# Passage to the feed-forward of a hybrid trunk layer: its sums and low parts on VectorE, recorded behind the scaling of the last row tile

## The chip, the cores and the metric

The kernel runs on one core of a Trainium2 chip. The metric is the device time of one execution in microseconds (us). The trace names the engines PE (TensorE matmul), PEld (TensorE weight load), DVE (VectorE), ACT (ScalarE), POOL (GpSimd) and SP (SyncE, which here issues the DMAs). Each engine works through its own list of instructions in order; an instruction that waits for another engine holds back all that stands behind it in its own list.

## What is computed

One trunk layer on x, 1024 rows (tokens) by 1024 columns, float32. Two mixers run first (a differential attention and an mLSTM); then comes the part that matters here:

```python
x = x + jnp.concatenate([attn_out, mlstm_out], axis=-1) @ w_out[l]

h2 = rms_norm(x, ffn_norm_g[l])
x = x + (jax.nn.silu(h2 @ w_gate[l]) * (h2 @ w_up[l])) @ w_down[l]
return rms_norm(x, final_norm_g)
```

The "passage" is the stretch from the last row tiles of `x + ... @ w_out` to the first products of `h2 @ w_gate` and `h2 @ w_up`.

## The kernel before

Every float32 product is made of three matmuls on two halves: a "high part" (the float32 value cast to float32r, a copy on ACT, L107) and a "low part" (the value less its high part, a subtraction, L108). `split(hi, lo, src, eng)` emits the two; `eng` is the engine of the subtraction, DVE unless POOL is named.

**Row tiles.** The 1024 rows are 8 tiles of 128. The output projection `out_proj` takes them in the order 0, 1, 2, 3, 4, 7, 6, 5. For each tile it runs 48 matmuls of 128x512 (24 into each half of the columns, tile name `dwo`, L1111 to L1113), adds x on DVE (`x1`, L1117), squares and sums the row on ACT (L1137), takes the reciprocal root on POOL (`ssq`, L1138, and `rs`, L104), and scales the row on DVE (`h2`, L1141). PE then transposes `h2` (L1047) into the operand of the feed-forward; DVE (L1053) and ACT (L1056) take the transposed tile out of PSUM with the norm's gain. For tile 5, the last, the transposes are named `th2l` and stand in PE's list behind the first 24 matmuls of the feed-forward.

**The feed-forward's first product is a seven-product scheme** (Strassen-Winograd, `unit`). With the transposed `h2` cut into four blocks (columns in halves, rows in halves), its seven right-hand operands are b11 and b21 (rows 0 to 511), b22 and b12 (rows 512 to 1023) and sums t1 = b12-b11, t3 = b22-b12, t2 = b22-t1 and t4 = b21-t2. Each is 128x4x512 and needs a high and a low part. Blocks of rows 0 to 511 are in `hst`, of rows 512 to 1023 in `h2r`.

- `t_slices(c)` makes the 128-row slice c of t1, t3 and b22 as soon as row tile c+4 is transposed: two subtractions on DVE (`tt`, `h2r`) and three splits (five DVE-sized instructions in all, and three ACT copies). Tiles 4, 7, 6 and 5 give slices 0, 3, 2 and 1.
- `t_sums(c)` turns slice c of `hst` into t2 and t4 in place, with two instructions.
- For the first two slices made (0 and 3; `TP = 2`) the low parts and the sums are on POOL; so are two of four low parts of b21 (`B21 = 2`) and those of t4.

**The units.** `unit` runs seven steps on a weight tile `st`: step 1 uses b11, 2 b21, 5 t1, 6 t2, 7 t3, 4 t4, 3 b22. A step is 12 matmuls (`mul12`, L186 to L188), and needs its weights split too (`w`) and, for some, sums of weight quarters on DVE (`st`, L214 to L235). The first two units (gate and up, `two`) are interleaved, so a step takes 24 matmuls: first step 1 of both, then the transposes `th2l`, then steps 2 and 5 of both, and so on. A matmul of step 5 reads all 512 columns of t1, which is all four slices.

**What sets the order.** PE's list is written by hand here (`manual_schedule`). The lists of DVE, ACT and POOL are set by a scheduler that places each instruction where it expects the engine to be free; `tc.high_priority()` moves instructions ahead, and `tc.issue_after(i)` keeps instructions behind instruction i.

Of the kernel before, what the change touches and what calls it, by code (L numbers as in the profile page):

```python
# [14 lines left out]
ALU = mybir.AluOpType  # L15
# [16 lines left out]
ML_K = 128 ** -0.5  # L32
RING, RING_A, RING_F = 9, 5, 7
AHEAD = 2
TP = 2
B21 = 2
XT = 4
M_POOL = (1, 2)
UO = (0, 1, 3, 2, 4, 5, 6, 7)
# [16 lines left out]
LATE = (10, 13, 6, 9)  # L56
# [3 lines left out]
LAST = DONE[-1]  # L60
SLICES = [i - 4 for i in DONE if i >= 4]
# [3 lines left out]
def block_kernel(ctx, tc, x, xT, pos, cols, gate_b, lam_in, w_vg, w_mo, w_qk, w_dv,  # L65
                 w_out, w_gu, w_dn, fng, out):
    nc = tc.nc
    act, dve, pool, pe, sp = nc.scalar, nc.vector, nc.gpsimd, nc.tensor, nc.sync
# [37 lines left out]
    def split(hi, lo, src, eng=None):  # L106
        act.copy(hi, src)  # L107
        (eng or dve).tensor_sub(lo, src, hi.bitcast(F32))  # L108
# [14 lines left out]
    def ring_tile(ringb, n_all, n=512):  # L123
        i = ring_n[0] % n_all
        ring_n[0] += 1
        w = (ringa if i < RING_A else ringb).tile([P, 2, 520], F32R, tag="w", name="w")
        return w[:, 0, 0:n], w[:, 1, 0:n]
# [27 lines left out]
    def drain(gen):  # L155
        for _ in gen:
            pass
# [230 lines left out]
    with ExitStack() as pa:  # L388
# [3 lines left out]
        with ExitStack() as pm:  # L392
# [80 lines left out]
            for n in range(4):  # L473
                for a in range(2):
# [5 lines left out]
            t1, t2, t3 = ([tq.tile([P, 4, 512], F32R, tag=f"t{n}{hl}", name=f"t{n}{hl}") for hl in range(2)]  # L480
                          for n in (1, 2, 3))
# [529 lines left out]
        while not done:  # L1011
            u, st = next(steps)
# [8 lines left out]
    b12, b22 = h2r  # L1021
    pb = ctx.enter_context(ExitStack())
    bw = pb.enter_context(tc.tile_pool(name="b_work", bufs=2, reuse_waits="tile"))
    H, hst, late_c, td_pool = {}, [], [], [psd]

    def t_slices(c):
        cs = slice(c * P, (c + 1) * P)
        p1, p2 = b12[:, :, cs], b22[:, :, cs]
        tt = bw.tile([P, 4, P], F32, tag="tt", name="tt", bufs=1)
        dve.tensor_sub(tt, p1, hst[0][:, :, cs])  # L1030
        eng = pool if c in SLICES[:TP] else dve
        split(H["t1"][0][:, :, cs], H["t1"][1][:, :, cs], tt, eng)
        dve.tensor_sub(p1, p2, p1)
        split(H["t3"][0][:, :, cs], H["t3"][1][:, :, cs], p1, eng)
        split(H["b22"][0][:, :, cs], H["b22"][1][:, :, cs], p2, eng)

    def t_sums(c):
        cs = slice(c * P, (c + 1) * P)
        eng = pool if c in SLICES[:TP] else dve
        eng.tensor_tensor(hst[0][:, :, cs], hst[0][:, :, cs], b12[:, :, cs], op=ALU.add)  # L1040
        eng.tensor_tensor(hst[1][:, :, cs], hst[1][:, :, cs], hst[0][:, :, cs], op=ALU.subtract)

    def h2_out(i, h2, ps_tile, gs=(0, 1)):
        for g in gs:
            tp = ps_tile()
            for j in range(4):
                pe.transpose(tp[:, j, :], h2[:, (4 * g + j) * P:(4 * g + j + 1) * P], ident)  # L1047
            if i < 4:
                dst = bw.tile([P, 4, P], F32, tag="tt", name="ht", bufs=1)
            else:  # L1050
                dst = h2r[g][:, :, (i - 4) * P:(i - 3) * P]
            if g == 0:
                dve.tensor_tensor(dst, tp, gffn[:, 0:4].unsqueeze(2).broadcast_to([P, 4, P]), op=ALU.mult)  # L1053
            else:
                for j in range(4):
                    act.mul(dst[:, j], tp[:, j], gffn[:, 4 + j:5 + j])  # L1056
            if i < 4:
                sp.dma_start(h2_d[g][:, :, i * P:(i + 1) * P], dst)
                n_h2[0] += 1
        if i >= 4 and 1 in gs:  # L1060
            if hst:
                t_slices(i - 4)
            else:
                late_c.append(i - 4)

    def d_tile():
        return td_pool[0].tile([P, 4, P], F32, tag="d", name="td")

    def out_proj():
        prev = nxt = None  # L1070

        def load(i):
            mt = bw.tile([P, 8, P], F32, tag="mt", name="mt", bufs=1)
            mf = mt.rearrange("p h e -> p (h e)")
            sp.dma_start(mf[:, 0:256], mx_da[i])
            if i != LAST:
                sp.dma_start(mf[:, 256:512], mx_db[i])
            sp.dma_start(mf[:, 512:1024], mx_ml[:, i, :])
            x1 = bw.tile([P, S], F32, tag="x1", name="x1")
            sp.dma_start(x1, x[i * P:(i + 1) * P, :])  # L1080
            return [i, x1, mt, {}, 0, tm[0]]

        def poll():
            nonlocal nxt
            if nxt is None:
                if ready:
                    nxt = load(ready.pop(0))
                return
            nxt[4] += 1
            if nxt[4] in nxt[5][:2]:  # L1090
                g = 1 if nxt[4] == nxt[5][0] else 0
                tp = d_tile()
                for j in range(4):
                    src = mt_last[:, j - 2, :] if nxt[0] == LAST and 4 * g + j in (2, 3) else nxt[2][:, 4 * g + j, :]
                    pe.transpose(tp[:, j, :], src, ident)
                nxt[3][g] = [v.rearrange("p (j e) -> p j e", e=P) for v in ring_tile(None, RING_A)]
                split(*nxt[3][g], tp)

        while True:
            poll()  # L1100
            if nxt is None or nxt[4] < nxt[5][1]:
                yield 0 if nxt is None else None
                continue
            (i, x1, _, mm, _, th), nxt = nxt, None
            for u in range(2):
                us = slice(u * 512, (u + 1) * 512)
                ps = psd.tile([P, 512], F32, tag="d", name="dwo")
                for n_, k in enumerate((4, 5, 6, 7, 0, 1, 2, 3)):
                    mh, ml = (v[:, k % 4, :] for v in mm[k // 4])
                    wh, wl = (wo[hl, k // 4, u][:, k % 4] for hl in range(2))  # L1110
                    pe.matmul(ps, mh, wh, start=(n_ == 0), stop=False)  # L1111
                    pe.matmul(ps, mh, wl, start=False, stop=False)  # L1112
                    pe.matmul(ps, ml, wh, start=False, stop=(n_ == KC - 1))  # L1113
                    poll()
                    if n_ == KC - 1:
                        with tc.high_priority():
                            dve.tensor_add(x1[:, us], ps, x1[:, us])  # L1117
                    if prev and 8 * u + n_ in th[2:]:
                        g = th[2:].index(8 * u + n_)
                        h2_out(*prev, d_tile, (g,))  # L1120
                        if g:
                            prev = None
                            if i == LAST:
                                t_sums(SLICES[2])
                    yield
                if u == 0 and i == LAST:
                    for n, g in (("b11", 0), ("b21", 1)):
                        H[n] = [slots.tile([P, 4, 512], F32R, tag=f"A{hl}{g}", name=n) for hl in range(2)]
                        for q in range(4):
                            split(H[n][0][:, q], H[n][1][:, q], hst[g][:, q], pool if g and q < B21 else dve)  # L1130
                    for c in SLICES[:2]:
                        t_sums(c)
            ssq = bw.tile([P, 1], F32, tag="ssq2", name="ssq2")
            sp.dma_start(x1_d[i], x1)
            with tc.high_priority():
                h2 = bw.tile([P, S], F32, tag="h2", name="h2", bufs=1)
                act.activation(h2, x1, AF.Square, accum_out=ssq)  # L1137
                pool.tensor_scalar(ssq, ssq, 1.0 / S, EPS, op0=ALU.mult, op1=ALU.add)  # L1138
                rs = bw.tile([P, 1], F32, tag="rs", name="rs")
                rsqrt_of(rs, ssq)  # L1140
                dve.tensor_scalar_mul(h2, x1, rs)  # L1141
            prev = (i, h2)
            if i == LAST:
                out_last.append(prev)
                return

    out_last, tm, n_h2 = [], [(TM0, TM1) + TH], [0]
    f_ = out_proj()
    for u, st in steps:
        if st == 0:  # L1150
# [24 lines left out]
        sp.dma_start(hst[g], h2_d[g])  # L1175
    for c in late_c:
        t_slices(c)
    drain(f_)
    px.close()
    pps.close()  # L1180
# [40 lines left out]
        next(u)  # L1221
    with tc.high_priority():
        h2_out(*out_last[0], lambda: tl.pop())
    pb.close()
    ringc = ctx.enter_context(tc.tile_pool(name="ringc", bufs=RING_F - RING_A, reuse_waits="tile"))
    pfw = ExitStack()
    fw[0] = pfw.enter_context(tc.tile_pool(name="f_work", bufs=2, reuse_waits="tile"))
    for _ in range(2):
        for u in two:
            next(u)  # L1230
    t_sums(SLICES[3])
    for n, g in (("t2", 0), ("t4", 1)):
        H[n] = [slots.tile([P, 4, 512], F32R, tag=f"B{hl}{g}", name=n) for hl in range(2)]
        for q in range(4):
            split(H[n][0][:, q], H[n][1][:, q], hst[g][:, q], pool if g else dve)
    phs.close()
    ssp = ctx.enter_context(tc.tile_pool(name="ssp", bufs=1, side="right", reuse_waits="tile"))
    raw = {}
# [168 lines left out]
    for step in SEQ_D:  # L1407
        _, wq, q = STEP[step]
# [93 lines left out]
```

## Time and profile before

| | us |
|---|---|
| three runs | 1229.0, 1231.23, 1232.24 (median 1231.23) |
| the profiled execution, its own time | 1228.96 |
| its span in the trace | 1226.8 |

| engine | busy us | share of the span | instructions |
|---|---|---|---|
| PE | 1186.7 | 97% | 5692 |
| DVE | 862.2 | 70% | 1437 |
| ACT | 530.0 | 43% | 1114 |
| POOL | 276.6 | 23% | 212 |

The span runs from the first instruction to the last; 2.2 us of the execution lie around it. The passage lies between 530 and 600 us of the span. A time in a row is counted from the span's start. "Idle before" in brackets is how long the engine had nothing to do before an instruction, and behind the arrow is what ended it.

### The profile page before, as it was taken

What the parts mean: (1) busy time and instruction counts of PE and PEld (TensorE: products, weight loads), DVE (VectorE), ACT (ScalarE), POOL (GpSimd) and SP (SyncE); (2) the same over time, 40 slices, a digit from 0 to 9 for tenths busy, and PEclk for the clock granted to TensorE, in tenths of its full rate; (3) what the DMA queues carried; (4) which work ended last, traced back from release to release, by engine and by line L of the source; (5) the groups of instructions that cost most, each with busy time, mean ns of one, the idle gap of its engine ahead of it and who ended that gap; (6) DMA issues with size and microseconds to landing.
All of it is one profiled execution on the core that took longest, in us unless ns stands there. A gap on an engine that the chain in (4) does not pass through costs nothing.

```text
span 1226.8 us, 15931 instructions
## 1 busy us (share of the span) xinstructions
PE 1186.7 (97%) x5692; PEld 975.9 (80%) x5692; DVE 862.2 (70%) x1437; ACT 530.0 (43%) x1114; POOL 276.6 (23%) x212
## 2 busy tenths in 40 slices
PE   9899999899998999997999999999999999999997
PEld 7678877898886888886888888888888888888886
DVE  8667868854767767739866767676666778775674
ACT  4933344325557554735533233322333245344453
POOL 3145877401133100025121100111011102000000
PEclk9989999999999999999999999999999999999999
DMA  9368641421478334060132312323133268723241
GB/s 334 99 196 221 191 156 69 164 113 52 146 219 287 122 126 141 31 245 34 69 129 96 128 65 99 129 95 121 43 129 113 111 235 303 294 95 105 84 163 69
DMA packets 87727, 172.37 MB, mean 141 GB/s; under 512 B 10208, under 2 KB 43104, under 8 KB 81248
## 3 DMA queue, kind: packets, MB, share of 16 engines
q1 hardware_dynamic: 86032, 169.76, 40.4%
q10 hardware_dynamic: 1616, 1.59, 0.4%
q8 instruction: 45, 0.74, 0.2%
q14 instruction: 34, 0.28, 0.1%
HBM read 117.58 MB, written 53.74 MB: 140 GB/s over the span
## 4 chain that ended last, share of the span: by engine, by line
PE 77%; DVE 5%; POOL 5%; issue 5%; ACT 4%; DMA 4%; SPq 0%; ACTq 0%; POOLq 0%; DVEq 0%
PE g L186 13%; PE g L187 13%; PE g L188 13%; PE y L1419 6%; PE y L1418 6%; PE y L1420 6%; PE to L333 2%; PE dwo L1113 2%; PE dwo L1112 2%; PE dwo L1111 2%; DVE w L108 1%; PE s L290 1%; PE tat L325 1%; PE s L291 1%; DVE xt L583 1%
## 5 line engine op out<-in xcount | busy, mean ns | idle before, releaser
L107 ACT CAST w<-st 128x512 fp32r<-128x512 f32 x218 | 133.0, 619 | 272.2 <-PE g L188 121.9
L108 DVE TENSOR_TENSOR w<-st,w 128x512 fp32r<-128x512 f32 x203 | 160.8, 797 | 104.1 <-ACT w L107 103.0
L186 PE MATMUL g<-t,w 128*128 128x512 f32 x448 | 178.0, 397 | 0.0
L187 PE MATMUL g<-t,w 128*128 128x512 f32 x448 | 177.1, 395 | 0.0
L188 PE MATMUL g<-t,w 128*128 128x512 f32 x448 | 176.3, 393 | 0.0
L1419 PE MATMUL y<-fhl,w 128*128 128x512 f32 x308 | 122.0, 396 | 0.0
L1418 PE MATMUL y<-fhl,w 128*128 128x512 f32 x308 | 121.7, 395 | 0.0
L1420 PE MATMUL y<-fhl,w 128*128 128x512 f32 x308 | 120.8, 392 | 0.0
L187 PE MATMUL g<-b,w 128*128 128x512 f32 x264 | 104.8, 397 | 0.0
L186 PE MATMUL g<-b,w 128*128 128x512 f32 x264 | 104.2, 395 | 0.0
L188 PE MATMUL g<-b,w 128*128 128x512 f32 x264 | 104.0, 394 | 0.0
L186 PEld LDWEIGHTS g<-t,w 128*128 128x128 f32 x448 | 84.2, 188 | 22.9 <-DVE u L224 3.0
L188 PEld LDWEIGHTS g<-t,w 128*128 128x128 f32 x448 | 84.2, 188 | 20.3
L187 PEld LDWEIGHTS g<-t,w 128*128 128x128 f32 x448 | 84.3, 188 | 19.1
L1203 POOL TENSOR_TENSOR ss<-sg 128x512 f32<-128x512 f32 x11 | 17.3, 1575 | 354.5 <-DVE sg L1201 354.5
L107 ACT CAST w<-gs 128x512 fp32r<-128x512 f32 x76 | 46.5, 619 | 70.0 <-PE y L1420 52.3
L108 DVE TENSOR_TENSOR w<-gs,w 128x512 fp32r<-128x512 f32 x76 | 53.6, 712 | 29.5 <-ACT w L107 29.5
L1418 PEld LDWEIGHTS y<-fhl,w 128*128 128x128 f32 x308 | 57.8, 188 | 14.3
L108 DVE TENSOR_TENSOR fhl<-w,fhl 128x512 fp32r<-128x512 f32 x77 | 51.2, 698 | 25.5 <-ACT fhl L107 25.5
L1420 PEld LDWEIGHTS y<-fhl,w 128*128 128x128 f32 x308 | 57.9, 188 | 13.9
L1419 PEld LDWEIGHTS y<-fhl,w 128*128 128x128 f32 x308 | 57.9, 188 | 13.2
L107 ACT CAST fhl<-w 128x512 fp32r<-128x512 f32 x77 | 44.2, 618 | 45.4 <-PE y L1420 41.6
(358 smaller groups left out, 2666.7 us busy)
## 6 DMA issues: line engine op xcount, KB each, us to landing
st<-in_w_gu SPq DMA_DIRECT2D x22, 1024.0 KB
gs<-gm_d SPq DMA_DIRECT2D x76, 256.0 KB
gm_d<-sg SPq DMA_DIRECT2D x11, 1024.0 KB
w<-in_w_dn SPq DMA_DIRECT2D x44, 256.0 KB
gm_d<-ss SPq DMA_DIRECT2D x11, 768.0 KB
st<-in_w_qk SPq DMA_DIRECT2D x8, 1024.0 KB
qbuf<-q_d SPq DMA_DIRECT2D x64, 128.0 KB
q_d<-xt SPq DMA_DIRECT2D x24, 256.0 KB
```

The costliest lines, as they stand in the source:

```text
L107: act.copy(hi, src)
L108: (eng or dve).tensor_sub(lo, src, hi.bitcast(F32))
L186: pe.matmul(ps, w[0][:, ks], h[0][:, k, :], start=first and k == 0, stop=False, **sk)
L187: pe.matmul(ps, w[0][:, ks], h[1][:, k, :], start=False, stop=False, **sk)
L188: pe.matmul(ps, w[1][:, ks], h[0][:, k, :], start=False, stop=k == 3, **sk)
L333: pe.matmul(po[:, 0, :], at[:, j, :], dv[j // 4][:, j % 4, hh * P:(hh + 1) * P], start=(j == 0), stop=(j == i))
L1111: pe.matmul(ps, mh, wh, start=(n_ == 0), stop=False)
L1112: pe.matmul(ps, mh, wl, start=False, stop=False)
L1113: pe.matmul(ps, ml, wh, start=False, stop=(n_ == KC - 1))
L1418: pe.matmul(bk[q][b], gh, w[0], start=first and k == 0, stop=False, **sk)
L1419: pe.matmul(bk[q][b], gh, w[1], start=False, stop=False, **sk)
L1420: pe.matmul(bk[q][b], gl, w[0], start=False, stop=k == FH - 1, **sk)
```

## The change

Three things are changed, all in the passage.

- **Engines.** The 16 instructions of the passage that POOL had (low parts of slices 0 and 3, of two quarters of b21 and of t4, and the sums of slices 0 and 3) go to DVE.
- **Where slices are made.** While the last tiles are projected (`tm[0] == LATE`), `t_slices` is put off: the slices go into `late_c` and are emitted, with three `t_sums`, after `h2_out` of the last tile.
- **Order.** What is put off, and steps 2 and 5 of the first two units, are emitted under `tc.issue_after(scaled[0].ins)`: on each engine they stand behind the scaling of the last tile's rows (L1135 of the changed kernel).

```diff
@@ block_kernel @@
     def t_slices(c):
...
-        eng = pool if c in SLICES[:TP] else dve
-        split(H["t1"][0][:, :, cs], H["t1"][1][:, :, cs], tt, eng)
+        split(H["t1"][0][:, :, cs], H["t1"][1][:, :, cs], tt)
         dve.tensor_sub(p1, p2, p1)
-        split(H["t3"][0][:, :, cs], H["t3"][1][:, :, cs], p1, eng)
-        split(H["b22"][0][:, :, cs], H["b22"][1][:, :, cs], p2, eng)
+        split(H["t3"][0][:, :, cs], H["t3"][1][:, :, cs], p1)
+        split(H["b22"][0][:, :, cs], H["b22"][1][:, :, cs], p2)
     def t_sums(c):
         cs = slice(c * P, (c + 1) * P)
-        eng = pool if c in SLICES[:TP] else dve
-        eng.tensor_tensor(hst[0][:, :, cs], hst[0][:, :, cs], b12[:, :, cs], op=ALU.add)
-        eng.tensor_tensor(hst[1][:, :, cs], hst[1][:, :, cs], hst[0][:, :, cs], op=ALU.subtract)
+        dve.tensor_add(hst[0][:, :, cs], hst[0][:, :, cs], b12[:, :, cs])
+        dve.tensor_sub(hst[1][:, :, cs], hst[1][:, :, cs], hst[0][:, :, cs])
...
         if i >= 4 and 1 in gs:
-            if hst:
+            if hst and tm[0] != LATE:
                 t_slices(i - 4)
             else:
                 late_c.append(i - 4)
...
-                            if i == LAST:
-                                t_sums(SLICES[2])
                     yield
                 if u == 0 and i == LAST:
...
-                            split(H[n][0][:, q], H[n][1][:, q], hst[g][:, q], pool if g and q < B21 else dve)
-                    for c in SLICES[:2]:
-                        t_sums(c)
+                            split(H[n][0][:, q], H[n][1][:, q], hst[g][:, q])
...
-                dve.tensor_scalar_mul(h2, x1, rs)
+                scaled[0] = dve.tensor_scalar_mul(h2, x1, rs)
...
     with tc.high_priority():
         h2_out(*out_last[0], lambda: tl.pop())
+    with tc.issue_after(scaled[0].ins):
+        for c in late_c:
+            t_slices(c)
+        for c in SLICES[:3]:
+            t_sums(c)
...
     for _ in range(2):
         for u in two:
-            next(u)
+            with tc.issue_after(scaled[0].ins):
+                next(u)
     t_sums(SLICES[3])
...
-            split(H[n][0][:, q], H[n][1][:, q], hst[g][:, q], pool if g else dve)
+            split(H[n][0][:, q], H[n][1][:, q], hst[g][:, q])
```

The lists of PE and SP are the same in both kernels but for line numbers. What moved on POOL and DVE is shown here; names carry their buffer's number.

POOL's list around the last tile's `ssq2_5630` and `rs_5635` in the kernel before: b21's low parts, then the four sums of slices 0 and 3, then the reciprocal root of the last tile, then t4's low parts.

```order
L108 TENSOR_TENSOR b21_5571<-hst1_5277,b21_5570 128x512 x2
L1040 TENSOR_TENSOR hst0_5275<-hst0_5275,h2r0_3709 128x4x128 x2
L1041 TENSOR_TENSOR hst1_5277<-hst1_5277,hst0_5275 128x4x128 x2
L1138 TENSOR_SCALAR ssq2_5630<-ssq2_5630 128x1
L104 TENSOR_TENSOR rs_5635<-ssq2_5630,mhalf_110 128x1
L108 TENSOR_TENSOR t4_5793<-hst1_5277,t4_5792 128x512 x4
```

The same place in the changed kernel, from the tile before the last (`ssq2_5502`) to the first sums of the feed-forward's output (`ss`).

```order
L1132 TENSOR_SCALAR ssq2_5502<-ssq2_5502 128x1
L102 TENSOR_TENSOR rs_5507<-ssq2_5502,mhalf_110 128x1
L1132 TENSOR_SCALAR ssq2_5597<-ssq2_5597 128x1
L102 TENSOR_TENSOR rs_5602<-ssq2_5597,mhalf_110 128x1
L1198 TENSOR_TENSOR ss_5961<-sg_5952 128x512
```

Nothing of the passage but the reciprocal roots is left on POOL.

DVE's list in the kernel before, from the last addition of x (`x1_5430`) through the scaling of the last tile (`h2_5632`) to the low part of t1's last slice (`t11_5267<-tt_5698`, which step 5 needs).

```order
L1117 TENSOR_TENSOR x1_5430<-dwo_5584,x1_5430 128x512
L108 TENSOR_TENSOR t31_5269<-h2r0_3709,t30_5268 128x4x128
L108 TENSOR_TENSOR w_5747<-st_5645,w_5747 128x512
L1041 TENSOR_TENSOR hst1_5277<-hst1_5277,hst0_5275 128x4x128
L218 TENSOR_TENSOR st_5645<-st_5645 128x512
L1141 TENSOR_SCALAR h2_5632<-x1_5430,rs_5635 128x1024
L108 TENSOR_TENSOR w_5765<-st_5665,w_5765 128x512
L218 TENSOR_TENSOR st_5665<-st_5665 128x512
L1053 TENSOR_TENSOR h2r0_3709<-th2l_5644,colt_109 128x4x128
...
L1033 TENSOR_TENSOR h2r0_3709<-h2r1_3710,h2r0_3709 128x4x128
L108 TENSOR_TENSOR b221_5271<-h2r1_3710,b220_5270 128x4x128
L108 TENSOR_TENSOR t11_5267<-tt_5698,t10_5266 128x4x128
```

The same place in the changed kernel: the last low parts of b11, the last addition of x (`x1_5421`), the scaling (`h2_5599`), the first of what stands behind it, and the end of the row of slices.

```order
L106 TENSOR_TENSOR b11_5543<-hst0_5275,b11_5542 128x512 x4
L1115 TENSOR_TENSOR x1_5421<-dwo_5562,x1_5421 128x512
L1135 TENSOR_SCALAR h2_5599<-x1_5421,rs_5602 128x1024
L1028 TENSOR_TENSOR tt_5665<-h2r0_3709,hst0_5275 128x512
L106 TENSOR_TENSOR b221_5271<-h2r1_3710,b220_5270 128x4x128 x3
L106 TENSOR_TENSOR w_5714<-st_5612,w_5714 128x512
...
L1028 TENSOR_TENSOR tt_5692<-h2r0_3709,hst0_5275 128x512
L106 TENSOR_TENSOR t31_5269<-h2r0_3709,t30_5268 128x4x128
L1037 TENSOR_TENSOR hst1_5277<-hst1_5277,hst0_5275 128x4x128
L1030 TENSOR_TENSOR h2r0_3709<-h2r1_3710,h2r0_3709 128x4x128
L106 TENSOR_TENSOR t11_5267<-tt_5692,t10_5266 128x4x128
```

Between the scaling and t1's last low part, that low part counted in, stand 9 DVE instructions in the kernel before and 41 in the changed one; between the last addition of x and the scaling stand 4 before and none after. The 41 are 19 of the slices, 6 of `t_sums`, 8 sums of weight quarters, 7 low parts of weights and the taking out of `th2l`.

## Rows read from the trace of the kernel before

**Rows 1.** The page: busy time, share of the span, instructions.

```profile
PE 1186.7 (97%) x5692; PEld 975.9 (80%) x5692; DVE 862.2 (70%) x1437; ACT 530.0 (43%) x1114; POOL 276.6 (23%) x212
```

**Rows 2.** Waits of PE, 500 to 586: total us, times, longest.

```profile
PE th2l L1047 <- DVE h L1141: 5.3, 1, 5.3
PE td L1047 <- DVE h L1141: 1.1, 1, 1.1
```

**Rows 3.** Windows: stretch, us, busy by engine (instructions), PEclk, DMA share, GB/s.

```profile
570.00:580.00 10.00, 4.69 (x20) 3.81 (x20) 9.26 (x9) 3.73 (x8) 6.60 (x6) 0.86 0.13 52
586.00:700.00 114.00, 114.00 (x492) 91.98 (x491) 81.22 (x111) 38.15 (x65) 23.80 (x16) 1.00 0.29 107
```

**Rows 4.** Timeline of PE: start, us, engine, line, operation, count, idle before.

```profile
557.88 0.40 PE L1113 MATMUL dwo<-wo,w 128*128 128x512 f32 x1
559.39 0.63 PE L1047 MATMUL td<-ident,h 128*128 128x128 f32 x4 [1.11 <-DVE h L1141]
...
566.34 0.39 PE L1113 MATMUL dwo<-wo,w 128*128 128x512 f32 x1
...
571.92 0.39 PE L188 MATMUL g<-b,w 128*128 128x512 f32 x1
577.61 1.97 PE L1047 MATMUL th2l<-ident,h 128*128 128x128 f32 x8 [5.31 <-DVE h L1141]
579.23 0.78 PE L186 MATMUL g<-b,w 128*128 128x512 f32 x1
...
580.63 0.40 PE L186 MATMUL g<-b,w 128*128 128x512 f32 x1
...
585.75 0.39 PE L187 MATMUL g<-t,w 128*128 128x512 f32 x1
```

**Rows 5.** Timeline of POOL in the passage.

```profile
557.34 3.04 POOL L108 TENSOR_TENSOR b<-hst,b 128x512 fp32r<-128x512 f32 x2
566.42 5.79 POOL L1040 TENSOR_TENSOR hst<-hst,h2r 128x512 f32<-128x512 f32 x2 [6.04 <-DVE b L108]
572.17 3.38 POOL L1041 TENSOR_TENSOR hst<-hst,hst 128x512 f32<-128x512 f32 x2
575.64 0.51 POOL L1138 TENSOR_SCALAR ssq<-ssq 128x1 f32<-128x1 f32 x1
...
589.16 5.96 POOL L108 TENSOR_TENSOR t<-hst,t 128x512 fp32r<-128x512 f32 x4 [12.39 <-ACT t L107]
```

**Rows 6.** Timeline of ACT: the squares of the last tile's rows.

```profile
570.04 1.06 ACT L1137 ACTIVATE h<-x 128x1024 f32<-128x1024 f32 x1 [1.92 <-issue]
```

**Rows 7.** Timeline of DVE in the passage.

```profile
541.42 0.68 DVE L1117 TENSOR_TENSOR x<-dwo,x 128x512 f32<-128x512 f32 x1
544.29 0.75 DVE L1141 TENSOR_SCALAR h<-x,rs 128x1024 f32<-128x1024 f32 x1 [2.19 <-POOL rs L104]
...
557.48 1.77 DVE L1141 TENSOR_SCALAR h<-x,rs 128x1024 f32<-128x1024 f32 x1
...
569.27 0.68 DVE L1117 TENSOR_TENSOR x<-dwo,x 128x512 f32<-128x512 f32 x1
...
572.68 1.75 DVE L1041 TENSOR_TENSOR hst<-hst,hst 128x512 f32<-128x512 f32 x1
...
576.80 0.75 DVE L1141 TENSOR_SCALAR h<-x,rs 128x1024 f32<-128x1024 f32 x1 [0.71 <-POOL rs L104]
...
578.19 0.69 DVE L218 TENSOR_TENSOR st<-st 128x512 f32<-128x512 f32 x1
...
582.41 0.68 DVE L108 TENSOR_TENSOR t<-tt,t 128x512 fp32r<-128x512 f32 x1
...
588.43 0.68 DVE L108 TENSOR_TENSOR w<-st,w 128x512 fp32r<-128x512 f32 x1
```

**Rows 8.** Timeline of PE at the kernel's start: its first large matmuls.

```profile
5.12 0.79 PE L142 MATMUL po<-w,hT 128*128 128x512 f32 x1 [0.58 <-ACT hT L111]
...
10.40 0.47 PE L142 MATMUL po<-w,hT 128*128 128x512 f32 x1
```

More of the change, by code (lines that the diff above doesn't have):

```diff
@@ L34 @@
 AHEAD = 2
-TP = 2
-B21 = 2
 XT = 4
@@ L1067, in d_tile @@
         return td_pool[0].tile([P, 4, P], F32, tag="d", name="td")
+    scaled = [None]
     def out_proj():
@@ L1177, in block_kernel @@
         t_slices(c)
+    late_c.clear()
     drain(f_)
```

## The prediction

> **What bounds the kernel now.** The page comes first: PE is busy for 97% of the span [rows 1], so only time that PE loses or wins counts, and a wait of PE is paid in full. Next come PE's waits in the passage: two only, 5.3 us ahead of the last tile's transposes (`th2l`) and 1.1 us ahead of those of the tile before [rows 2]. From 586 to 700 PE has no idle time at all, 492 matmuls in 114 us, 0.232 us each [rows 3]; whatever is lost in the passage is not won back there.
>
> The timelines tell why PE waits. It is done with step 1 of the first two units at 572.3 (571.92 and 0.39) and goes on at 577.61 [rows 4]. The scaling that it waits for runs at 576.80 [rows 7]. The squares behind it were summed on ACT by about 571.2 [rows 6], but POOL, which takes the root, was in the four sums of `hst` from 566.42 until 575.55, and began `ssq` only at 575.64 [rows 5]. DVE had been late as well: the last matmul of the output projection ends at 566.73 [rows 4], and x is added at 569.27 [rows 7]. After the wait PE is slow: in the stretch 570 to 580 its granted clock is 0.86 [rows 3], and `th2l` and the next three matmuls take 3.02 us, 577.61 to 580.63 [rows 4].
>
> **What the change takes away.** POOL keeps nothing of the passage but the roots, and DVE nothing between the last addition of x and the scaling.
>
> The wait at tile 6 (1.11 us [rows 4]) was a scaling of 1.77 us instead of 0.75, beside POOL's b21 low parts [rows 5, 7]. With these gone from POOL, even from the same start, 557.48, it ends at 558.2, when PE's matmul of 557.88 ends too (558.3); I take the wait to go whole, and all of PE's later work to move 1.11 us ahead. The output projection then ends at 566.73 - 1.11 = 565.6.
>
> At the last tile an undisturbed passage is seen at tile 7: x is added at 541.42, the scaling starts at 544.29, ends at 545.04 [rows 7], which is 2.87 and 3.62 us later. So the changed kernel adds x at 565.7 and scales from 568.5 to 569.3. PE, done with step 1 at 572.3 - 1.11 = 571.2, finds `h2` ready; the 5.31 us go.
>
> The slow clock behind that wait goes too. The transposes took 1.62 us and the three matmuls 1.40 [rows 4]; at full clock the matmuls would take 3 x 0.232 = 0.70, and the transposes half, 0.81. That is 1.5 us.
>
> Together 1.1 + 5.3 + 1.5 = 7.9 us are won. PE would run `th2l` from 571.2 to 572.0 and step 2 of both units (24 x 0.232 = 5.6 us) until about 577.6; a weight's low part, fifth behind the scaling on DVE, may hold step 2 by 0.4 us, which the next wait swallows.
>
> **What it puts in.** Step 5 needs t1, high and low, of all four slices. Before, most of it was finished about when PE left the projection, and between the scaling and the last low part of t1 stood 9 DVE instructions, that one counted in; it ran at 582.41, and step 5 (its first low product at 585.75) came later than that and waited for nothing [rows 4, 7]. In the changed kernel 41 stand there. They are subtractions and additions of 128x512 float32, and the row that is nearest is DVE's own in the same passage: from 578.19 to 588.43 it ran 17 of the same kind back to back in 10.24 us, 0.602 each [rows 7], with POOL idle (12.39 us until 589.16 [rows 5]). That is also the cost of the 16 that come over from POOL, where they took 1.5 to 2.9 us each [rows 5]; off PE's path the change is a saving.
>
> The first of the 41 starts 0.7 us behind the scaling's start, at 569.2. The last starts 40 x 0.602 = 24.1 us later, at 593.3, and ends at 594.0. The first low product of step 5 then runs at 594.0 instead of 585.75: **8.3 us later**. PE stands still from 577.6 until then, 16.4 us, instead of 5.3, and must start from the slow clock as it did behind the 5.3. I take the same 1.5 us for that; the bounds are 0 and 2.5 (the kernel's first twelve large matmuls took 5.28 us, 5.12 to 10.40, where 2.8 is due [rows 8]).
>
> Check by the ledger: 16.4 + 1.5 - 7.9 = 10.0; by the clock times: 8.3 + 1.5 = 9.8. I take **+9.8 us**.
>
> Is anything late behind step 5? t2 stands 7 DVE instructions behind t1's last (4.2 us), under the 5.6 us of step 5; t3 is finished before that, and t4 (four instructions, formerly POOL's) is read three steps later. So no. Nothing is given back either: PE has no idle time there now [rows 3].
>
> Bounds of DVE's share: if every one of the 41 has to wait for a copy of ACT or a semaphore, each takes its whole 0.68 instead of 0.602 [rows 7], 3.2 us more; a gain below 0.602 has no row for two-operand work here, its case is the second rival. With the clock's bounds the forecast's own range is +8.3 to +14.
>
> **Rivals.** *The gain alone (faster).* The wait for t1 would have to be hidden: PE wins 7.9 us and the 16 instructions are cheaper on DVE. That gives 1228.96 - 7.9 = 1221.1 for the profiled execution, 1223.3 against the median. It decides on how many of the 41 must be done when step 2 ends at 577.6: from 569.2 at 0.602 that is 14, and with some 24 the change breaks even. For it speaks that POOL's long row of sums is what PE's longest wait came from [rows 5]; against it that the 41 are counted in the list itself, and that a matmul reads all 512 columns of t1. Chance 0.05.
>
> The Trainium skill (GPSIMD Engine Reference, Engine selection) advises VectorE over GpSimd for elementwise work on two inputs, as GpSimd is about twice as slow; by that rule alone the change would be a gain of this size. The rows of this case agree on the price (1.5 us and more against 0.602), but the rule says nothing on who waits for the engine that takes the work.
>
> *DVE is quicker once POOL is quiet (no change).* The scaling runs 1024 columns in 0.75 us [rows 7], 0.375 per 512. At that rate the 41 take 15.4 us, t1 is ready at 584.7, PE waits 7.1 us, and 7.1 + 1.5 - 7.9 = +0.7 gives 1229.7, 1231.9 against the median. The 17 back-to-back instructions beside an idle POOL speak against it. Chance 0.05.
>
> The Trainium skill (VectorE: DVE Perf Modes, Why `tensor_tensor` can't do 2×_2P or 4×) says that the doubled rate belongs to instructions with one tensor input, since a second one takes the second read port; no row here shows a float32 subtraction at that rate, which agrees.
>
> *Copies of ACT hold the row (slower still).* ACT's copies stand in its own list behind copies that wait for PE and for DVE; a t1 copy that comes late stops DVE, and all behind it. At most points the list leaves two or more DVE instructions between a source and the low part that needs its copy, enough for one copy. The price is the 3.2 us above and up to 2.5 for the clock: 1241 to 1243, some 1245 against the median. Chance 0.15.
>
> **How the numbers follow.** The profiled execution took 1228.96 us, its span 1226.8, and stands 2.3 us below the median of the runs, 1231.23. The sum gives 1238.8 against the profiled execution and 1231.23 + 9.8 = 1241.0 against the median; I forecast the latter. The chance of the forecast is 0.75. The range takes in the forecast's own (+8.3 to +14, 1239.5 to 1245.2) and the runs' spread (2.2 below their median, 1.0 above), 1236 to 1246. A measurement of this kernel can tell about 0.3%, 3.7 us, from no change: faster 0.05, within 0.05, slower 0.90.
>
> **What the changed kernel's profile would show.** Right: no wait of PE at `td` and `th2l`; a wait of some 16 us at the first matmuls of t1, put down to DVE's low part of t1 or ACT's copy for it; DVE busy without a gap for 25 us behind the scaling, which ends near 569; POOL idle but for roots; no new idle time of PE behind that. Wrong: a PE wait below 6 us at t1, a DVE pitch well off 0.60, or a scaling that still comes after 571.

## The result and the profile after

The changed kernel takes 1239.69 us (median of four runs, 1238.04 to 1242.58) where the kernel before takes 1230.18 (four runs): 9.5 us slower, ratio 1.0075 with a 95% interval of 1.0053 to 1.0097. The forecast was 9.8 us slower, 1241.0 (against the three runs then known, 1231.23). The profiled execution took 1238.04 us with a span of 1236.3.

On the page of the changed kernel's profile POOL lost 16 instructions and 26.6 us of busy time, DVE gained 16 instructions and only 0.9 us [rows 1].

```profile
PE 1184.2 (96%) x5688; PEld 974.0 (79%) x5692; DVE 863.1 (70%) x1453; ACT 530.6 (43%) x1114; POOL 250.0 (20%) x196
```

PE's waits between 545 and 714 (what waited and for whom, total us, times, longest). Both waits of [rows 2] are gone; two others, at the first two matmuls of step 5, are there instead.

```profile
PE g L184 <- ACT t L105: 14.5, 1, 14.5
PE g L185 <- DVE t L106: 1.0, 1, 1.0
```

PE's timeline (start, us, engine, line, operation, shapes, count, idle before), to be laid beside [rows 4].

```profile
558.04 0.60 PE L1043 MATMUL td<-ident,h 128*128 128x128 f32 x4
...
570.76 1.03 PE L1043 MATMUL th2l<-ident,h 128*128 128x128 f32 x8
571.55 0.48 PE L184 MATMUL g<-b,w 128*128 128x512 f32 x1
...
577.04 0.40 PE L186 MATMUL g<-b,w 128*128 128x512 f32 x1
591.97 0.79 PE L184 MATMUL g<-t,w 128*128 128x512 f32 x1 [14.53 <-ACT t L105]
593.73 0.80 PE L185 MATMUL g<-t,w 128*128 128x512 f32 x1 [0.96 <-DVE t L106]
...
596.88 0.51 PE L186 MATMUL g<-t,w 128*128 128x512 f32 x1
597.23 0.39 PE L184 MATMUL g<-t,w 128*128 128x512 f32 x1
```

The transposes of tile 6 (558.04) and of tile 5 (570.76) start without a wait, those of tile 5 6.85 us earlier than before and at full clock. Step 2 is done at 577.44. Then PE has one matmul to do until 593.73. The eight matmuls from there to 597.23 take 3.50 us where 8 x 0.232 = 1.86 are due: 1.64 us of slow clock.

POOL's and DVE's timelines around the scaling show why the one wait went and the other came, to be laid beside [rows 5, 7]. POOL first: the root follows the squares at once.

```profile
567.39 0.19 POOL L1132 TENSOR_SCALAR ssq<-ssq 128x1 f32<-128x1 f32 x1 [10.77 <-ACT h L1131]
567.66 0.54 POOL L102 TENSOR_TENSOR rs<-ssq,mhalf 128x1 f32<-128x1 f32 x1
```

DVE: x is added at 565.38, the scaling runs at 568.24, the first of the 41 at 568.91 and the 41st, t1's last low part, at 592.99. That is 24.08 us for 40 steps, 0.602 each.

```profile
565.38 0.69 DVE L1115 TENSOR_TENSOR x<-dwo,x 128x512 f32<-128x512 f32 x1 [1.96 <-PE dwo L1111]
568.24 0.76 DVE L1135 TENSOR_SCALAR h<-x,rs 128x1024 f32<-128x1024 f32 x1 [2.17 <-POOL rs L102]
568.91 0.69 DVE L1028 TENSOR_TENSOR tt<-h2r,hst 128x512 f32<-128x512 f32 x1
...
592.99 0.68 DVE L106 TENSOR_TENSOR t<-tt,t 128x512 fp32r<-128x512 f32 x1
```

Windows (stretch, us, busy time and instructions of PE, PEld, DVE, ACT and POOL, granted clock, DMA share, GB/s), beside [rows 3]: PE does nothing from 580 to 590 while DVE is busy all the time; the clock is low until 597; from 600 on PE has no idle time and runs the same 492 matmuls in 114 us as before.

```profile
580.00:590.00 10.00, 0.00 (x0) 0.00 (x0) 10.00 (x18) 3.61 (x6) 0.00 (x0) 0.50 0.00 0
590.00:600.00 10.00, 7.07 (x21) 5.34 (x22) 9.46 (x17) 6.90 (x12) 0.00 (x0) 0.64 0.01 2
600.00:714.00 114.00, 114.00 (x492) 91.97 (x491) 80.77 (x112) 35.69 (x61) 17.82 (x12) 1.00 0.30 113
```

### The profile page after: what moved, and what is told of

Its sections match the earlier page's. It is cut to its first block, busy times and chain, and to the rows that moved or that the text cites. A ratio compares the mean times of both kernels' runs of the same rounds, so it can differ in the third digit from the quotient of the medians.

```text
span 1236.3 us, 15911 instructions
## 1 busy us (share of the span) xinstructions
PE 1184.2 (96%) x5688; PEld 974.0 (79%) x5692; DVE 863.1 (70%) x1453; ACT 530.6 (43%) x1114; POOL 250.0 (20%) x196
## 4 chain that ended last, share of the span: by engine, by line
PE 74%; DVE 8%; POOL 5%; DMA 5%; issue 5%; ACT 2%; SPq 1%; ACTq 0%; POOLq 0%; DVEq 0%
PE g L184 12%; PE g L185 12%; PE g L186 12%; PE y L1420 6%; PE y L1419 6%; PE y L1421 6%; PE dwo L1111 2%; PE dwo L1110 2%; PE dwo L1109 2%; PE to L331 2%; DVE w L106 2%; PE s L288 1%; PE tat L323 1%; PE s L289 1%; DVE xt L581 1%
## 5 line engine op out<-in xcount | busy, mean ns | idle before, releaser
L106 DVE TENSOR_TENSOR w<-st,w 128x512 fp32r<-128x512 f32 x203 | 157.1, 780 | 104.4 <-ACT w L105 103.3
```

## The experiments

The change has three parts: the engines (POOL's 16 instructions to DVE), the putting-off of the slices, and the hold of steps 2 and 5 behind the scaling. The experiments take them apart. The theory tested, Q, is the prediction's: step 5 waits until DVE has worked off what stands between the scaling and t1's last low part. The rivals are W, that 16 more instructions of 0.60 us on DVE are 9.6 us of loss wherever they stand (a sum that happens to equal the result), and H, that the hold is the loss.

The profiled executions start the passage at different times: tile 7's transposes begin between 544.6 and 549.4 in the nine traces, though PE's work up to there is the same (DVE's and POOL's lists part some 8 us earlier, with the first slice; the 400 matmuls ahead of these transposes take 66.9 us in each). So a single span says less than the passage itself. The table measures it in two pieces: from the first transposes of tile 7 to step 5's first low product, and from there to the first matmul of the down product (`y`); from `y` to the end all nine take 222 us. Its last columns are the sum against the kernel before, and the ratio of the timed runs. "Row" is the number of DVE instructions from the scaling to t1's last low part, that one counted in.

| kernel | row | to step 5, us | step 5 to `y`, us | sum against before, us | ratio, 95% interval |
|---|---|---|---|---|---|
| before | 9 | 40.5 | 419.2 | 0 | 1 |
| changed | 41 | 48.6 | 420.7 | +9.6 | 1.0075 (1.0053 to 1.0097) |
| engines alone | 10 | 38.9 | 419.4 | -1.4 | 0.9972 (0.9958 to 0.9986) |
| engines; slices early, three sums late | 15 | 35.6 | 421.0 | -3.1 | 0.9962 (0.9945 to 0.9980) |
| engines and putting-off, no hold | 33 | 44.1 | 422.1 | +6.5 | 1.0028 (1.0014 to 1.0042) |
| changed, sums behind t1 | 35 | 45.1 | 420.9 | +6.3 | 1.0042 (1.0025 to 1.0059) |
| engines and hold, slices early | 20 | 36.3 | 421.8 | -1.6 | 0.9976 (0.9963 to 0.9990) |
| putting-off and hold, POOL kept | 31 | 50.7 | 422.0 | +12.9 | 1.0095 (1.0082 to 1.0108) |
| t1 first | 9 | 32.7 | 420.6 | -6.4 | 0.9938 (0.9921 to 0.9955) |

The sums come from one execution each, the ratios from several. For two kernels the sum lies outside the interval of the ratio: "engines alone" (-1.4, where the interval is -5.2 to -1.7 us) and "no hold" (+6.5, where it is +1.7 to +5.2). So a sum is good to a microsecond or two; the sign agrees everywhere.

### Engines alone

The kernel before with POOL's 16 instructions on DVE and nothing else.

```diff
-TP = 2
-B21 = 2
+TP = 0
+B21 = 0
...
-            split(H[n][0][:, q], H[n][1][:, q], hst[g][:, q], pool if g else dve)
+            split(H[n][0][:, q], H[n][1][:, q], hst[g][:, q])
```

> The kernel before with one part of the change alone: the 16 instructions of the passage that POOL had go to VectorE; slices are made as early as before, nothing is held behind the scaling. Theory Q (the row behind the scaling sets the start of step 5): here 10 VectorE instructions lead from the scaling to t1's last low part (9 before, 41 changed), so step 5 waits for nothing; POOL's sums no longer delay the root, but 8 VectorE instructions stand between the last addition of x and the scaling, so PE still waits some 3 us at th2l. About 4 to 5 us faster than before, 1225 to 1227. Rival W (the work itself is the loss: 16 instructions of 0.60 us more on VectorE, 9.6 us): as slow as the changed kernel, 1239 to 1241. Rival H (the hold on steps 2 and 5 is the loss): faster than before, 1222 to 1228.

Measured: 1229.25 us against 1231.72, ratio 0.9972; less of a gain than expected, and clear of W. PE's timeline shows the wait at `th2l` down from 5.31 to 3.51 us, and a slow clock that goes on through the matmul of 584.13, not for 3 us as before but for some 5.5. DVE's timeline has the scaling only at 578.14, behind eight instructions.

```profile
578.95 1.97 PE L1047 MATMUL th2l<-ident,h 128*128 128x128 f32 x8 [3.51 <-DVE h L1141]
...
584.13 0.59 PE L188 MATMUL g<-b,w 128*128 128x512 f32 x1
```

```profile
578.14 0.75 DVE L1141 TENSOR_SCALAR h<-x,rs 128x1024 f32<-128x1024 f32 x1 [0.70 <-POOL rs L104]
```

So 16 more instructions on DVE are no loss: W falls. The waits that went are worth 2.9 us here (1.1 at tile 6, 1.8 at `th2l`); the longer slow clock takes some 1.2 of them back (2.7 us of loss instead of 1.5).

### Slices early, steps not held

The changed kernel with putting-off and hold undone; three of the sums stay behind the scaling.

```diff
-            if hst and tm[0] != LATE:
+            if hst:
...
-            with tc.issue_after(scaled[0].ins):
-                next(u)
+            next(u)
```

> The changed kernel with two parts undone: slices are made during the last projections again, and steps 2 and 5 are not held behind the scaling; the engines are as changed, and three of the sums stay behind the scaling. Theory Q: 15 VectorE instructions from the scaling to t1's last low part, 9 us from 569 on; step 5 starts near 580 instead of 585.7 (before) and 593.7 (changed), PE waits some 2.5 us there and nowhere else. About 6 us faster than before, 1223 to 1226. Rival W: 1239 to 1241. Rival H: 1222 to 1228.

Measured: 1227.12 us, ratio 0.9962. Step 5 starts 5.0 us earlier in the passage than before, as Q says within 1 us; 1.9 us of that are lost behind it, 1.7 of them to the clock. PE's timeline shows three short waits: 0.50 us at `th2l`, which was not expected, and 0.59 and 1.26 at step 5. Behind them matmuls take 0.63 us until 586.04, at half clock; the window of 584 to 586 has the granted clock, 0.50.

```profile
573.42 1.09 PE L1043 MATMUL th2l<-ident,h 128*128 128x128 f32 x8 [0.50 <-DVE h L1135]
...
580.70 0.50 PE L184 MATMUL g<-t,w 128*128 128x512 f32 x1 [0.59 <-ACT t L105]
582.45 0.50 PE L185 MATMUL g<-t,w 128*128 128x512 f32 x1 [1.26 <-DVE t L106]
...
583.05 0.63 PE L184 MATMUL g<-t,w 128*128 128x512 f32 x1
...
586.04 0.56 PE L185 MATMUL g<-t,w 128*128 128x512 f32 x1
```

```profile
584.00:586.00 2.00, 2.00 (x6) 1.56 (x5) 2.00 (x5) 1.98 (x5) 0.00 (x0) 0.50 0.00 0
```

### The hold undone

The changed kernel without `issue_after` on steps 2 and 5 (the second half of the diff above, alone); the slices stay put off.

> The changed kernel with one part undone: steps 2 and 5 of the first two units are not held behind the scaling; slices are still put off, engines as changed. Theory Q: 33 VectorE instructions instead of 41 from the scaling to t1's last low part, 8 x 0.60 = 4.8 us less, of which some go ahead of the scaling; step 5 starts near 589.5, PE waits some 12 us and restarts at half clock (1.5 us). 4 to 5 us slower than before, 4 to 5 us faster than changed: 1234 to 1236. Rival W: 1239 to 1241. Rival H: 1222 to 1228.

Measured: 1236.12 us against 1231.72. The row is 33 long, and DVE's timeline has the scaling at 570.24 and t1's last low part at 590.17: 19.93 us for 33 steps, 0.60 each. Both pieces of the passage together are 6.5 us longer than before, 3.1 us shorter than changed. H falls: without the hold the loss is smaller, but it is there. The hold adds to it by the eight instructions that it puts into the row (41 against 33).

```profile
570.24 0.75 DVE L1135 TENSOR_SCALAR h<-x,rs 128x1024 f32<-128x1024 f32 x1 [0.78 <-POOL rs L102]
...
590.17 0.69 DVE L106 TENSOR_TENSOR t<-tt,t 128x512 fp32r<-128x512 f32 x1
```

PE waits 9.76 us and then 0.96 at step 5, and the slow clock behind them costs 2.7 us here where it cost 1.6 in the changed kernel.

```profile
589.15 0.80 PE L184 MATMUL g<-t,w 128*128 128x512 f32 x1 [9.76 <-ACT t L105]
590.91 0.80 PE L185 MATMUL g<-t,w 128*128 128x512 f32 x1 [0.96 <-DVE t L106]
```

### The sums behind t1

The changed kernel with six DVE instructions moved from ahead of t1's last low part to behind it. The work, the engines and the hold are the same.

```diff
-        (eng or dve).tensor_sub(lo, src, hi.bitcast(F32))
+        return (eng or dve).tensor_sub(lo, src, hi.bitcast(F32))
...
-        split(H["t1"][0][:, :, cs], H["t1"][1][:, :, cs], tt)
+        t1_lo[0] = split(H["t1"][0][:, :, cs], H["t1"][1][:, :, cs], tt)
...
+    with tc.issue_after(t1_lo[0].ins):
         for c in SLICES[:3]:
             t_sums(c)
```

> The changed kernel with its six sums of slices 0, 3 and 2 moved behind t1's last low part; nothing else changes, the same instructions run on the same engines. Theory Q: 35 instead of 41 VectorE instructions in the row, 6 x 0.60 = 3.6 us less at t1, some 0.4 us of it lost again at t2: step 5 starts near 590.3, 3 us faster than changed, 1236 to 1237. Rivals W and H: as the changed kernel, 1239 to 1241.

Measured: 1237.03 us; the passage is 3.3 us shorter than in the changed kernel, and the piece ahead of step 5 is 3.4 us shorter. Six instructions of 0.602 are 3.6. DVE has the scaling at 569.20 and t1's last low part at 590.50.

```profile
569.20 0.75 DVE L1135 TENSOR_SCALAR h<-x,rs 128x1024 f32<-128x1024 f32 x1 [2.17 <-POOL rs L102]
...
590.50 0.69 DVE L106 TENSOR_TENSOR t<-tt,t 128x512 fp32r<-128x512 f32 x1
```

PE waits 12.12 us for t1 instead of 14.53 and 0.96.

```profile
590.52 0.80 PE L184 MATMUL g<-t,w 128*128 128x512 f32 x1 [12.12 <-ACT t L105]
591.24 0.79 PE L185 MATMUL g<-t,w 128*128 128x512 f32 x1
```

This is the run that tells Q from W and H most plainly: nothing is added or taken away, six instructions change places, and PE starts step 5 earlier by about as much. The trace tells it; by the timed runs alone (1.0042 against 1.0075) the two intervals still overlap.

### The hold kept, slices early

The changed kernel with the putting-off alone undone (the first half of the diff of "Slices early").

> The changed kernel with the putting-off alone undone: slices are made during the last projections again; steps 2 and 5 and three of the sums stay held behind the scaling, engines as changed. Theory Q (PE's step 5 waits until VectorE has worked off, at 0.60 us each, what stands between the scaling and t1's last low part): 20 instructions there, 12 us; step 5's first low product 3 us earlier than before, PE waits about 1 us at step 2 and 4 us at step 5, and the clock, which fell behind waits of this size in the runs so far, costs 1.5 to 3 us: 0 to 2 us faster than before. Rival W (16 more instructions on VectorE cost 9.6 us wherever they stand): 9 to 10 us slower than before.

Measured: 1227.08 us against 1230.27, ratio 0.9976; by the passage 1.6 us faster than before and 11.2 us faster than the changed kernel. The putting-off is the part that loses, and H falls again, since the hold is kept here. The row is 20 long, 12.10 us. PE waits 1.69 and 1.86 us and then runs at half clock (matmuls 0.63 us long) until 586.97.

```profile
568.84 0.76 DVE L1135 TENSOR_SCALAR h<-x,rs 128x1024 f32<-128x1024 f32 x1 [1.57 <-POOL rs L102]
...
580.94 0.69 DVE L106 TENSOR_TENSOR t<-tt,t 128x512 fp32r<-128x512 f32 x1
```

```profile
579.32 0.49 PE L184 MATMUL g<-t,w 128*128 128x512 f32 x1 [1.69 <-ACT t L105]
581.68 0.80 PE L185 MATMUL g<-t,w 128*128 128x512 f32 x1 [1.86 <-DVE t L106]
...
586.97 0.44 PE L185 MATMUL g<-t,w 128*128 128x512 f32 x1
```

### POOL kept

The changed kernel with the engines alone undone.

```diff
-        split(H["t1"][0][:, :, cs], H["t1"][1][:, :, cs], tt)
+        eng = pool if c in SLICES[:TP] else dve
+        split(H["t1"][0][:, :, cs], H["t1"][1][:, :, cs], tt, eng)
...
-        dve.tensor_add(hst[0][:, :, cs], hst[0][:, :, cs], b12[:, :, cs])
-        dve.tensor_sub(hst[1][:, :, cs], hst[1][:, :, cs], hst[0][:, :, cs])
+        eng = pool if c in SLICES[:TP] else dve
+        eng.tensor_tensor(hst[0][:, :, cs], hst[0][:, :, cs], b12[:, :, cs], op=ALU.add)
+        eng.tensor_tensor(hst[1][:, :, cs], hst[1][:, :, cs], hst[0][:, :, cs], op=ALU.subtract)
...
```

> The changed kernel with the engines alone undone: POOL keeps the 16 instructions; slices are put off and steps 2 and 5 are held, as changed. Theory Q: 31 VectorE instructions instead of 41 in the row, 6 us less if POOL does not disturb them (step 5's first low product near 587.5 in the frame of before's 585.75, some 3 to 5 us slower than before in all); beside POOL's tensor work VectorE's instructions took up to 1.75 us instead of 0.68, ten such POOL instructions would put up to 10 us on top (13 us slower than before). Rival W: without the 16 instructions on VectorE no loss, within 1 us of before.

Measured: 1242.01 us against 1230.27, ratio 1.0095; the slowest of all, with 16 fewer instructions on DVE than the changed kernel. The row has 31 instructions but takes 26 us, and PE waits 17.17 us for t1.

```profile
595.21 0.80 PE L186 MATMUL g<-t,w 128*128 128x512 f32 x1 [17.17 <-ACT t L107]
```

Beside POOL's tensor work, from 578.85 to 585.5, DVE's instructions follow each other by 1.68 instead of 0.60, one for one with POOL's:

```profile
578.85 1.75 DVE L1033 TENSOR_TENSOR h2r<-h2r,h2r 128x512 f32<-128x512 f32 x1
580.53 1.75 DVE L108 TENSOR_TENSOR b<-h2r,b 128x512 fp32r<-128x512 f32 x1
```

```profile
578.34 1.71 POOL L1041 TENSOR_TENSOR hst<-hst,hst 128x512 f32<-128x512 f32 x1
580.02 1.71 POOL L108 TENSOR_TENSOR t<-tt,t 128x512 fp32r<-128x512 f32 x1
```

W falls again, and the change's own first part shows as a gain: with slices put off and steps held, moving the 16 instructions to DVE brings 3.4 us by the passage (12.9 against 9.6; the timed ratios, 1.0095 and 1.0075, differ the same way, but their intervals overlap).

The Trainium skill (SBUF — State Buffer, SBUF: two separate sides) says that GpSimd and a VectorE instruction with two SBUF inputs share a pair of ports, that whichever starts first has it for its whole instruction, and that the other is blocked until then; the rows of 1.7 us agree. In the kernel before the same neighbours shared otherwise: POOL's two sums from 566.42 on took 2.9 us each [rows 5], while DVE went on at 0.60, five steps from 566.26 to 569.27 [rows 7]. What decides between the two is not shown here.

```profile
566.26 0.68 DVE L1033 TENSOR_TENSOR h2r<-h2r,h2r 128x512 f32<-128x512 f32 x1
```

### t1 first

A version from what the runs showed: engines as changed, slices early, no hold. The sums stand behind t1's last low part, those for t2 first, those for t4 behind t2's low parts; one split (t3's part of slice 2) that was ahead of the last scaling goes behind t1 too. `t_sums(c, g)` now makes one of its two sums, t2's for `g` 0 and t4's for `g` 1.

```diff
-            if hst and tm[0] != LATE:
+            if hst:
...
-    with tc.issue_after(scaled[0].ins):
-        for c in late_c:
-            t_slices(c)
-        for c in SLICES[:3]:
-            t_sums(c)
+    with tc.issue_after(t1_lo[0].ins):
+        cs = slice(SLICES[2] * P, (SLICES[2] + 1) * P)
+        split(H["t3"][0][:, :, cs], H["t3"][1][:, :, cs], b12[:, :, cs])
...
-            with tc.issue_after(scaled[0].ins):
-                next(u)
-    t_sums(SLICES[3])
+            next(u)
+    last_lo = t1_lo[0]
...
+        with tc.issue_after(last_lo.ins):
+            for c in SLICES:
+                t_sums(c, g)
+            for q in range(4):
+                last_lo = split(H[n][0][:, q], H[n][1][:, q], hst[g][:, q])
```

> A version from what the runs showed: engines as changed; slices made early, nothing held behind the scaling but one low part and its copy; the sums stand behind t1's last low part, those of t2 first, those of t4 behind t2's low parts. Theory Q: 4 VectorE instructions between the last addition of x and the scaling, 9 from it to t1's last low part, 25 to t2's last: PE waits for nothing in the passage, so the clock does not fall: from before 1.1 + 5.3 + 1.5 = 8 us are won, 1222 to 1224 where before takes 1231. Rival W: 9 to 10 us slower than before.

Measured: 1222.21 us against 1230.27, ratio 0.9938 (0.9921 to 0.9955): faster than both kernels. The transposes and step 5 start without a wait, the granted clock stays at 1.00, and the piece up to step 5 is 7.8 us shorter than before, which agrees with the 7.9 us that the prediction had put down as the gain.

```profile
570.54 1.09 PE L1046 MATMUL th2l<-ident,h 128*128 128x128 f32 x8
...
577.29 0.39 PE L185 MATMUL g<-t,w 128*128 128x512 f32 x1
```

```profile
570.00:580.00 10.00, 10.00 (x48) 8.04 (x47) 9.96 (x17) 6.10 (x13) 0.00 (x0) 1.00 0.01 2
580.00:590.00 10.00, 10.00 (x44) 8.09 (x44) 10.00 (x18) 7.51 (x13) 0.00 (x0) 1.00 0.00 0
```

Behind step 5 it loses 1.5 us against before. Two new waits of PE for a DVE addition make 1.0 of it, the longer one 0.90 at 619.89; where the rest comes from is open.

```profile
619.89 0.50 PE L184 MATMUL g<-t,w 128*128 128x512 f32 x1 [0.90 <-DVE u L222]
```

## Why the prediction was right

- **The waits that go.** Forecast: the wait at tile 6 whole (1.1 us), and the scaling of tile 5 from 568.5 so that the transposes start without a wait at 571.2. Measured: no wait at either, the scaling at 568.24, the transposes at 570.76, step 2 done at 577.44 (577.6). The weight's low part held step 2 by at most 0.16 us (0.4 was allowed): from 571.55 to 577.04 it makes 23 steps in 5.49 us, where 5.33 are due. The 7.9 us of gain stand alone in "t1 first": 7.8.
- **The row.** Forecast: 41 instructions at 0.602 us, t1's last low part starting at 593.3, step 5's first low product at 594.0. Measured: 24.08 us for the 40 steps, 592.99 and 593.73. The price per instruction was taken from a stretch of 17 in the kernel before and held, with 0.60 to 0.62 per instruction, in rows of 9 to 41; where POOL disturbed DVE (31 of them in 26 us) it did not.
- **The clock.** Forecast: 1.5 us for the restart, between 0 and 2.5. Measured 1.64 in the changed kernel, but 1.5 to 2.7 over all runs in which the clock fell. That it came out so near to 1.5 was luck in part: the prediction carried over the loss behind one wait, and the size of the wait does not set it (see the last section). The upper bound was too low.
- **Nothing given back.** From 600 on PE has no idle time, and 492 matmuls take 114.00 us as before.
- **The sum.** 8.3 + 1.5 = 9.8 us; the passage is 8.05 us longer to step 5 and 1.5 us longer behind it, 9.6. The timed runs give 9.5, with an interval of 6.5 to 11.9.
- **The rivals.** "The gain alone" is what a DVE list with 9 instead of 41 gives; the engines part taken alone or undone is a gain of 1.4 to 3.4 us by the passage. "DVE is quicker once POOL is quiet" did not happen: 0.602 throughout. "Copies of ACT hold the row" did not either: DVE has no idle time among the 41. PE's wait is put down to ACT's copy for t1 for 14.53 us, but that copy waited for DVE's `tt`, four places ahead in the same row.

## What to carry to other kernels

When work is put off so that a critical instruction finds its engine free, count what then stands between that instruction and the next thing that the bound engine needs, at the measured pitch of one instruction: the wait was moved, not removed. Here 41 x 0.60 us of row stood against the 8.5 us that PE still had to do (568.91 to 577.44), and the 15.5 us of waiting that were left outweighed the 6.4 us that went. Work that fills an engine while it would idle ahead of the critical instruction should stay there, and what stands behind it should be sorted by when the bound engine reads it (t1, then t2, then t4), which gained 0.6% against the kernel before with the same work. Moving elementwise work off the engine that contends was good here by itself; it was its order that lost.

## What the runs showed of the hardware

The clock fell behind waits much shorter than those of the kernel before, and what it cost did not follow the length of the wait. The loss is read from PE's timelines: the time that the matmuls behind the wait took until they were back at full pace, less 0.232 us for each of them (0.81 for the eight transposes).

| waits of PE, us | run | loss by the slow clock, us |
|---|---|---|
| 0.59 and 1.26 | slices early, steps not held | 1.7 |
| 1.69 and 1.86 | the hold kept, slices early | 2.6 |
| 3.51 | engines alone | 2.7 |
| 5.31 | before [rows 4] | 1.5 |
| 9.76 and 0.96 | the hold undone | 2.7 |
| 12.12 | the sums behind t1 | 1.7 |
| 14.53 and 0.96 | changed | 1.6 |
| 17.17 and 0.45 | POOL kept | 2.5 |

One wait of 1.11 us by itself (tile 6 in the kernel before, ended at 559.39 [rows 4]) and one of 0.90 (t1 first, ended at 619.89) left the granted clock at 1.00. The windows behind them, before first:

```profile
560.00:570.00 10.00, 10.00 (x47) 8.13 (x46) 10.00 (x17) 6.03 (x13) 3.96 (x2) 1.00 0.00 1
```

```profile
620.00:630.00 10.00, 10.00 (x44) 8.08 (x45) 5.31 (x9) 4.39 (x8) 0.00 (x0) 1.00 0.25 83
```

What sets the size of the loss is not shown.
